# Differential attention scores: the correction product taken over 128 rows in place of 64

## The chip, the core and the metric

The kernel runs on one core of one Trainium2 chip. The metric is the device time of one execution in microseconds (us). Engines are named as in the profile: PE is TensorE's matmuls, PEld its loads of the stationary operand, DVE is VectorE, ACT is ScalarE, POOL is GpSimd, SP is the queue that issues the DMAs. Lines such as L643 are lines of the kernel before, unless it is said that they are of the changed one.

## What is computed

One layer of a streaming encoder over 1024 tokens of 1024 channels. A common projection of the normalised input feeds a convolution branch, gated linear attention, and differential attention; their gated sum goes through an output projection, and a SwiGLU follows. The change lies in differential attention alone: 8 heads, each with two score maps over 64 channels, subtracted after the softmax.

```
s  = einsum('bqhtd,bkhtd->bhtqk', qi, k) * HD ** -0.5      # t = 0, 1: two maps of a head, d = 64
s  = where(key_chunk <= q_chunk, s, -inf)                  # block-causal, chunks of 64
p  = softmax(s)
pd = p[:, :, 0] - lam * p[:, :, 1]
o  = einsum('bhqk,bkhv->bqhv', pd, v)
```

## The kernel before

Products that need more than the short matmul format (fp32r) are taken in two parts: an operand is split into an upper part `hi` (a cast on ACT) and the rest `lo` (a subtraction on DVE), and `mm3` (L114) adds hi·hi, hi·lo and lo·hi into one PSUM bank. Nearly all of PE's work is of this kind: three matmuls per step of K, each with its own load of a 128x128 stationary block, and 512 or 256 moving columns.

Token mixing walks through weight units of 256 columns (`units`, L43). A unit's projection is a generator that yields after 8 or so products; at each yield `tick` (L198) resumes other work that is due: pieces of weight splitting, convolution taps, and the attention cores. So the scores and values of head h stand on PE between the projections of the units that come after it. The times at which an attention core goes on are counted in ticks (`LAG`, `SPACE`, L63 to L65), not in us. The tile framework then sets the final order on every engine by its own cost estimates and places the semaphores, so one more instruction on one engine can move others.

`diff_qk` (L572) makes a head's operands. The 128 output channels of a projection are map 0 (rows 0 to 63, `L`) and map 1 (rows 64 to 127, `H`). For map 0 the tile `q0` holds the upper part of q in rows `L` and its lower part in rows `H`; `k0` holds the upper part of k in both halves. One product over 128 rows gives (q_hi + q_lo)·k_hi. For map 1 it is the same with the halves exchanged. The lower part of k lies in one tile `klo`: map 0's in rows `L`, map 1's in rows `H`. Four casts on ACT (L591 to L594) and two subtractions on DVE (L595, L596) make it for each half of the tokens, from one PSUM bank of the ring `pb` (four banks).

`diff_core` (L620) goes through the 8 blocks of 128 queries; block qb sees (qb + 1)·128 keys. `softmax` (L627) computes the scores of both maps: per map and stretch of columns, one product over 128 rows with `k` (L642), and a second over 64 rows that adds q_hi·k_lo (L643). Blocks 0 to 3 have one stretch a map, blocks 4 to 7 two. Then DVE masks and takes the maxima (L645 to L649), ACT the exponentials with their sums (L651, first into `p`, the second in place), DVE forms the difference `p` (L653 to L656). Later `turn` (L660) transposes it on PE (L667) and ACT copies it out (L669), and `values` (L673) multiplies with v (L678). The scores use the PSUM ring `sc`, two tiles of two banks; blocks 4 to 7 take both at once.

Of the kernel before, what the change touches and what calls it, by code (L numbers as in the profile page):

```python
# [8 lines left out]
F32R = mybir.dt.float32r  # L9
U8 = mybir.dt.uint8  # L10
AF = mybir.ActivationFunctionType
ALU = mybir.AluOpType
# [4 lines left out]
P = 128  # L17
S = 1024
# [22 lines left out]


def units():  # L43
    """Order in which the 256-column weight units are consumed."""
    out = []
    for h in range(NH):
        out += [("CV", 2 * h), ("A", h), ("V", h), ("CV", 2 * h + 1), ("OG", h)]
        if h < NH - 1:
            out += [("MG", h)]
    for j in range(ND // 2):  # L50
        out += [("DV", j), ("QK", 2 * j), ("MD", j), ("QK", 2 * j + 1)]
    out += [("MG", NH - 1)] + [("MC", u) for u in range(4)]
    out += [("PW", u) for u in range(4)]
    out += [("WO", u) for _ in range(2) for u in range(4)]
    for j in range(FT // 2):
        out += [("FG", j), ("FU", j)]
    out += [("FO", j) for j in range(FT // 2)]
    return out
# [9 lines left out]
def body(nc, tc, I, out):  # L68
    x_d, w_d, wf_d, wfup_d, par_d, lq_d, cst_d, msk_d, ffg_d, fng_d = I
    vec, act, pe, pool, sp = nc.vector, nc.scalar, nc.tensor, nc.gpsimd, nc.sync  # L70
# [7 lines left out]
    mix = tc.alloc_tile_pool(name="mix", bufs=1)  # L78
# [8 lines left out]
    one = cst[:, 2 * P:2 * P + 1].broadcast_to([P, P])  # L87
# [19 lines left out]
    def f(ap):  # L107
        return ap.bitcast(F32)
# [8 lines left out]
        pe.matmul(o, al, bh, start=False, stop=stop, skip_group_check=more)  # L117

    def rstd(dst, ss, n, width):
        """dst = (ss / n + eps) ** -0.5"""  # L120
        vec.tensor_scalar(out=dst, in0=ss, scalar1=1.0 / n, scalar2=EPS, op0=ALU.mult, op1=ALU.add)
        pool.tensor_tensor(out=dst, in0=dst, in1=mhalf[:, 0:width], op=ALU.pow)  # L122

    # ---- weights: stream of units, one ahead of its use, split in pieces behind the products
    ready = deque()
    state = {"n": 0, "gen": None}

# [44 lines left out]
    def wk(w, k, c=slice(0, 256)):  # L172
        return tuple(p[:, k % 2 * 256 + c.start:k % 2 * 256 + c.stop] for p in w[k // 2])

    # ---- work that runs behind the projections: generators, each yields after how many
    # parts of a projection (8 products) it goes on
    events, clock = [], {"now": 0, "seq": 0, "conv": 0.0}
    convq = deque()

# [26 lines left out]
    def run(gen):  # L206
        for _ in gen:
            tick()
# [3 lines left out]
            clock["now"] = max(clock["now"], events[0][0])  # L212
            resume()

    # ---- hidden state, transposed: [channel, token] in two exact parts
    def transposed(src, hh, hl, half, gcol):
        for k in range(KT):
            if half == 0 and k >= 4:
# [39 lines left out]
    def hs(half):  # L258
        return slice(half * HALF, (half + 1) * HALF)

    # ================= RMSNorm of x, transposed
    q4 = lambda name="q4": mix.tile([P, S + 32], F32, tag="q4", name=name, bufs=10)
    hset = bigset(big, "big", "h")
    xs = [q4("xt")[:, 0:D] for _ in range(NT)]
# [40 lines left out]
            if _ % 2:  # L305
                yield 1

    # ================= low-rank forget gate: rows 32 j to 32 j + 15 get h @ W_f with the
    # upper part of W_f, the next 16 rows that with its lower part
    ws = q4("ws").bitcast(F32R)  # L310
    wu, sst = ws[0:96, 0:HALF], ws[:, HALF:2 * HALF]
    fl4 = q4("fl").bitcast(F32R)
# [14 lines left out]
    spawn(x_rest(), 4)  # L327
    spawn(low_rank(1), 9)

    # ---- lambda of the differential attention, and its norm's weights  # L330
    lq = mix.tile([P, 256], F32, tag="h2", name="lq", bufs=10)
    sp.dma_start(lq, lq_d)
    lam = cpool.tile([P, 8], F32, name="lam")
# [1 line left out]
    for j in range(2):  # L335
        vec.tensor_tensor(out=lt[:, j * 64:(j + 1) * 64], in0=lq[:, j * 128:j * 128 + 64],
                          in1=lq[:, j * 128 + 64:j * 128 + 128], op=ALU.mult)
# [5 lines left out]
    vec.tensor_scalar(out=lam[:, 5:6], in0=par[:, P_DN:P_DN + 1], scalar1=0.5 * (1.0 - LAMBDA_INIT), scalar2=None, op0=ALU.mult)  # L343
    dng = lam[:, 5:6]

    # ---- gates: sigmoid(x) = (1 + tanh(x / 2)) / 2; what a gate multiplies carries the half
    def sigmoid2(out_, x):
        act.activation(out_, x, AF.Tanh, scale=0.5)

    for c0, n in ((P_DW, KT * TAPS), (P_GN, 2)):  # L350
        vec.tensor_scalar(out=par[:, c0:c0 + n], in0=par[:, c0:c0 + n], scalar1=0.5, scalar2=None, op0=ALU.mult)

    # ================= A. convolution
    csum = q4("csum")[:, 0:S]

    def conv_taps(ct, up, acc):
# [27 lines left out]
            yield  # L384
        convq.append(conv_taps(ct, up, acc[:, 0:S]))

    # ================= B. gated linear attention
    e4 = lambda name: mix.tile([P, S], F32, tag="e4", name=name, bufs=2)
    h2 = lambda name, dt=F32R: mix.tile([P, HALF], dt, tag="h2", name=name, bufs=10)
    G = {}  # L390
# [175 lines left out]
                yield 1  # L566
        del G[h]

    # ================= C. differential attention
    A = {}  # L570

    def diff_qk(h):  # L572
        w = unit()
        a = A.setdefault(h, {})
        q0, q1, k0, k1, kl = (q4(n).bitcast(F32R) for n in ("q0", "q1", "k0", "k1", "klo"))
        a.update(q=(q0, q1), k=(k0, k1), kl=kl)
        L, H = slice(0, 64), slice(64, 128)
        for half in range(2):
            c = hs(half)
            o = yield from proj_t(w, 0, half, hset)  # L580
            raw = h2("qraw", F32)
            act.activation(raw, o, AF.Copy, scale=0.125)
            act.copy(q0[L, c], raw[L])
            act.copy(q1[H, c], raw[H])
            vec.tensor_tensor(out=q0[H, c], in0=raw[L], in1=f(q0[L, c]), op=ALU.subtract)
            vec.tensor_tensor(out=q1[L, c], in0=raw[H], in1=f(q1[H, c]), op=ALU.subtract)
            yield
        for half in range(2):
            c = hs(half)
            o = yield from proj_t(w, 1, half, hset)  # L590
            act.copy(k0[L, c], o[L])  # L591
            act.copy(k1[H, c], o[H])
            act.copy(k0[H, c], o[L])
            act.copy(k1[L, c], o[H])  # L594
            vec.tensor_tensor(out=kl[L, c], in0=o[L], in1=f(k0[L, c]), op=ALU.subtract)  # L595
            vec.tensor_tensor(out=kl[H, c], in0=o[H], in1=f(k1[H, c]), op=ALU.subtract)  # L596
            yield
        spawn(diff_core(h), 2)

# [20 lines left out]
    def diff_core(h):  # L620
        a = A[h]
        osb = mix.tile([P, NT, P], F32, tag="o4", name="osb", bufs=2)
        ss = mix.tile([P, 8], F32, tag="ss", name="ss", bufs=2)
# [3 lines left out]
        def softmax(qb):  # L627
            n = (qb + 1) * P
            t = slice(qb * P, (qb + 1) * P)
            st_ = mix.tile([P, 8], F32, tag="st", name="st", bufs=4)  # L630
            p0 = e4("p")
            b0 = 0
            if n <= HALF:
                s2 = bank2().rearrange("p (a b) -> p a b", a=2)
                sc = [s2[:, i, 0:n] for i in range(2)]
            else:
                b0 = P if n == HALF + P else 0
                sc = [bank2()[:, b0:b0 + n], bank2()[:, b0:b0 + n]]
            for i in range(2):
                L = slice(64 * i, 64 * i + 64)  # L640
                for c in (slice(0, min(n, HALF - b0)), slice(HALF - b0, n))[:1 + (n > HALF)]:
                    pe.matmul(sc[i][:, c], a["q"][i][:, t], a["k"][i][:, c], start=True, stop=False)  # L642
                    pe.matmul(sc[i][:, c], a["q"][i][L, t], a["kl"][L, c], start=False, stop=True)  # L643
                if n > HALF:
                    vec.memset(sc[i][0:64, n - 64:n], NEG)  # L645
                    vec.tensor_reduce(out=st_[:, i:i + 1], in_=sc[i], axis=AX.X, op=ALU.max, negate=True)
            if n <= HALF:
                vec.memset(s2[0:64, :, n - 64:n], NEG)
                vec.tensor_reduce(out=st_[:, 0:2], in_=s2[:, :, 0:n], axis=AX.X, op=ALU.max, negate=True)  # L649
            for i in range(2):  # L650
                act.activation((p0[:, 0:n], sc[1])[i], sc[i], AF.Exp, bias=st_[:, i:i + 1],  # L651
                               accum_out=st_[:, 2 + i:3 + i])
            vec.reciprocal(st_[:, 4:6], st_[:, 2:4])  # L653
            vec.tensor_scalar(out=st_[:, 6:7], in0=st_[:, 2:3], scalar1=st_[:, 5:6], scalar2=nlam,
                              op0=ALU.mult, op1=ALU.mult)
            vec.scalar_tensor_tensor(out=p0[:, 0:n], in0=sc[1], scalar=st_[:, 6:7], in1=p0[:, 0:n],  # L656
                                     op0=ALU.mult, op1=ALU.add)
            return p0, st_
# [24 lines left out]
        pend, parts, plan = {}, {}, []  # L683
# [50 lines left out]
                sp.dma_start(g_d[2 * u + c, :, hs(half)], sg)  # L734
                yield

    # From here on the tokens go in two parts: tiles 0, 1, 4, 5 and tiles 2, 3, 6, 7
    PARTS = ((0, 1, 4, 5), (2, 3, 6, 7))

    def part(ap, i):  # L740
# [2 lines left out]
    def pair(ap):  # L743
        return ap.rearrange("p (a c) -> p a c", a=2)

    # ================= convolution: LayerNorm over channels, swish
    def conv_norm(cs):
        csum = b4("csum")
        sp.dma_start(csum, s_d)
# [70 lines left out]
                spawn(conv_norm(us))  # L820
    drain()
    spawn(conv_split(1))
    # ================= pointwise convolution, gate, sum of the branches
    yset = bigset(keep, "kb", "y")

    def pointwise(u):
# [19 lines left out]
    for u in range(4):  # L846
        run(pointwise(u))

    # ================= output projection, residual, RMSNorm
    # The SwiGLU's first product is taken in 2 x 2 blocks (output columns and tokens, halves of K)  # L850
    # by Winograd's form of Strassen's algorithm: seven block products in place of eight.
    # right operands: "11", "21", "22" (blocks of h) and T1..T4 (their sums)
    B = {}
    x2 = {}
    ffg = b4("ffg")
# [71 lines left out]
    for half in range(2):  # L927
# [2 lines left out]
                block(name, keep, "kb")  # L930
        for u in range(4):
            run(out_proj(half, u))
    # ================= SwiGLU, first product
    NU = FT
    first = state["n"]
    block("T4", keep, "kb")
# [41 lines left out]
    right = ("11", "T1", "T2", "21", "T3", "T4", "22")  # L978
# [41 lines left out]
            hilo(B["T4"][0][:, k, :], B["T4"][1][:, k, :], u)  # L1020
            yield 3

    # the second product's operands
    mids, x3 = {}, {}

    def load_mid(j):
# [21 lines left out]
    for at, (n, p) in enumerate(order):  # L1048
# [15 lines left out]
        o = ch["abacaab"[p]]  # L1064
# [33 lines left out]
    drain()  # L1098
    fbs[0].release()

    # ================= SwiGLU, second product, residual, RMSNorm
    fc = tc.alloc_tile_pool(name="fc", bufs=1)
    fng = fc.tile([P, D], F32, tag="fng", name="fng")
    sp.dma_start(fng, fng_d)
# [105 lines left out]
```

## Time and profile before

| what | value |
|---|---|
| three timed runs | 2170.72, 2171.11, 2172.71 us; median 2171.11 |
| span of the profiled execution, its own time | 2171.2 us, 0.1 above the median |
| PE busy | 2147.5 us, 99% of the span |
| DVE, ACT busy | 1385.6 us (64%), 859.0 us (40%) |
| mean granted clock of TensorE | 0.998 of full speed, which is the level of 2.4 GHz |
| products of scores | 192 of L642 and 192 of L643, between 637.6 and 1218.2 us |

The busy time of PE says that it always has something in flight, not that it is at its peak: matmuls overlap, and their ends are modelled. What a product takes from the engine is read from the step, the time from its start to the start of the next one. Two views matter: the engine's instructions in order of time, and the groups by line.

### The profile page before, as it was taken

To read this page: it belongs to the slowest core of one execution; us is meant where nothing else is said; L and a number is where in the kernel's file an instruction comes from. 1 tells how busy PE (TensorE), PEld (TensorE's weight loads), DVE (VectorE), ACT (ScalarE), POOL (GpSimd) and SP (SyncE) were. 2 spreads that over 40 slices of the span, in tenths; PEclk is the share of its full clock that TensorE was granted. 3 is DMA by queue.
4 is the path that set the end of the run, shared out by engine and by line. 5 is a ranking of instruction groups with operands and counts; after the bars stand their busy time and mean duration, and the time that the engine had idled before them with its cause. 6 is when DMAs were issued, how large, how long until landed. Compare 5 with 4: busy or idle time off the path is not lost.

```text
span 2171.2 us, 27863 instructions
## 1 busy us (share of the span) xinstructions
PE 2147.5 (99%) x10988; PEld 1787.7 (82%) x10988; DVE 1385.6 (64%) x2088; ACT 859.0 (40%) x1729; POOL 45.5 (2%) x45
## 2 busy tenths in 40 slices
PE   8999999999999999999999999999999999999998
PEld 6988988889887878778777888898888888888886
DVE  5988798789755454454545356567755545576766
ACT  6342251342345455455545354234433333341212
POOL 0000000000000000000000000000000000000000
PEclk9999999999999999999999999999999999999999
DMA  4112112121121111110111265443322222282111
GB/s 159 39 59 68 59 41 77 49 74 55 48 78 30 49 44 40 35 59 25 59 35 53 71 241 165 131 140 122 107 89 78 92 73 81 85 292 97 59 39 78
DMA packets 65059, 177.65 MB, mean 82 GB/s; under 512 B 6720, under 2 KB 17600, under 8 KB 64928
## 3 DMA queue, kind: packets, MB, share of 16 engines
q1 hardware_dynamic: 64928, 175.88, 24.4%
q8 instruction: 86, 1.41, 0.3%
q14 instruction: 45, 0.37, 0.1%
HBM read 137.58 MB, written 38.27 MB: 81 GB/s over the span
## 4 chain that ended last, share of the span: by engine, by line
PE 95%; DVE 3%; DMA 1%; issue 0%; POOL 0%; ACT 0%; SPq 0%; DVEq 0%; POOLq 0%; ACTq 0%
PE pb L115 22%; PE pb L116 22%; PE pb L117 22%; PE sc L115 6%; PE sc L116 5%; PE sc L117 5%; PE sc L643 3%; PE pb L678 3%; PE sc L642 3%; PE pb L667 1%; POOL sm L122 0%; DVE wl L112 0%; DVE xn L1127 0%; PE pb L712 0%; PE pb L504 0%
## 5 line engine op out<-in xcount | busy, mean ns | idle before, releaser
L115 PE MATMUL pb<-h,wh 128*128 128x512 f32 x1152 | 462.8, 402 | 0.0
L117 PE MATMUL pb<-h,wl 128*128 128x512 f32 x1152 | 450.9, 391 | 0.0
L116 PE MATMUL pb<-h,wh 128*128 128x512 f32 x1152 | 450.6, 391 | 0.0
L111 ACT CAST wh<-wr 128x512 fp32r<-128x512 f32 x331 | 203.5, 622 | 394.4 <-DVE x L1119 122.1
L112 DVE TENSOR_TENSOR wl<-wr,wh 128x512 fp32r<-128x512 f32 x331 | 225.5, 688 | 165.3 <-ACT wh L111 163.4
L362 DVE SCALAR_TENSOR_TENSOR acc<-up,par,acc 128x1024 f32<-128x1024 f32 x240 | 307.1, 1280 | 2.7
L115 PEld LDWEIGHTS pb<-h,wh 128*128 128x128 f32 x1152 | 217.1, 188 | 48.3 <-issue 5.1
L117 PEld LDWEIGHTS pb<-h,wl 128*128 128x128 f32 x1152 | 216.6, 188 | 46.8
L116 PEld LDWEIGHTS pb<-h,wh 128*128 128x128 f32 x1152 | 217.0, 188 | 41.3 <-DVE h L228 0.9
L1119 DVE TENSOR_TENSOR x<-x,pb 128x512 f32<-128x512 f32 x176 | 120.0, 684 | 59.8 <-PE pb L117 59.2
L115 PE MATMUL pb<-wh,h 128*128 128x256 f32 x512 | 148.1, 289 | 0.0
L117 PE MATMUL pb<-wh,h 128*128 128x256 f32 x512 | 144.9, 283 | 0.0
L116 PE MATMUL pb<-wl,h 128*128 128x256 f32 x512 | 144.8, 283 | 0.0
L115 PE MATMUL sc<-bT,wh 128*128 128x512 f32 x352 | 137.0, 390 | 0.5 <-ACT bT L111 0.5
L116 PE MATMUL pb<-wl,mh 128*128 128x512 f32 x352 | 136.9, 389 | 0.0
L115 PE MATMUL pb<-wh,mh 128*128 128x512 f32 x352 | 136.9, 389 | 0.0
L117 PE MATMUL pb<-wh,ml 128*128 128x512 f32 x352 | 136.9, 389 | 0.0
L116 PE MATMUL sc<-bT,wh 128*128 128x512 f32 x352 | 136.8, 389 | 0.0
L117 PE MATMUL sc<-bT,wl 128*128 128x512 f32 x352 | 136.6, 389 | 0.0
L111 ACT CAST wh<-s 128x512 fp32r<-128x512 f32 x88 | 54.5, 621 | 129.5 <-PE sc L116 79.4
L115 PEld LDWEIGHTS pb<-wh,h 128*128 128x128 f32 x512 | 98.1, 192 | 1.2 <-issue 0.6
L116 PEld LDWEIGHTS pb<-wl,h 128*128 128x128 f32 x512 | 98.1, 192 | 0.3
(249 smaller groups left out, 3768.2 us busy)
## 6 DMA issues: line engine op xcount, KB each, us to landing
wr<-w_dram SPq DMA_DIRECT2D x176, 512.0 KB, 3.6
m_d<-t SPq DMA_DIRECT2D x44, 256.0 KB, 2.1
mr<-m_d SPq DMA_DIRECT2D x22, 512.0 KB, 5.5
y_d<-y SPq DMA_DIRECT2D x28, 256.0 KB, 2.0
xt<-x_dram SPq DMA_DIRECT2D x8, 512.0 KB, 5.4
c_d<-acc SPq DMA_DIRECT2D x8, 512.0 KB, 2.7
g_d<-sgc SPq DMA_DIRECT2D x16, 256.0 KB, 2.1
c<-c_d SPq DMA_DIRECT2D x8, 512.0 KB, 7.8
```

Of the source, the lines that this page charges most:

```text
L111: act.copy(hi, src)
L112: vec.tensor_tensor(out=lo, in0=src, in1=f(hi), op=ALU.subtract)
L115: pe.matmul(o, ah, bh, start=start, stop=False, skip_group_check=more)
L116: pe.matmul(o, ah, bl, start=False, stop=False, skip_group_check=more)
L117: pe.matmul(o, al, bh, start=False, stop=stop, skip_group_check=more)
L362: vec.scalar_tensor_tensor(out=acc, in0=up[:, j:j + S], scalar=w, in1=acc, op0=ALU.mult, op1=ALU.add)
L642: pe.matmul(sc[i][:, c], a["q"][i][:, t], a["k"][i][:, c], start=True, stop=False)
L643: pe.matmul(sc[i][:, c], a["q"][i][L, t], a["kl"][L, c], start=False, stop=True)
L667: pe.transpose(pt[:, i * P:(i + 1) * P], pd[:, (g0 + i) * P:(g0 + i + 1) * P], ident)
L678: pe.matmul(ov[:, 0:P], parts[k // 4][:, c], a["v"][:, k, :], start=k == 0, stop=k == nk - 1)
L1119: vec.tensor_tensor(out=xx, in0=xx, in1=o, op=ALU.add)
```

## The change

For each map the lower part of k is now held in both halves of the partitions, as the upper part is, so that the second product has the same rows as the first: (q_hi + q_lo)·k_lo over 128 rows. It adds the term q_lo·k_lo to the sum. The tile `klo` (1024 columns, of the ring `q4`) is replaced by `kl0` for map 0 in the same ring, and by `kl1` for map 1, which is one tile for all heads (two halves that alternate between heads) and takes one of the three buffers of the ring `v8`; that ring otherwise holds v. DVE makes four subtractions a half of the tokens in place of two. Other edits remove comments. Lines of the changed kernel are 3 or 4 higher from L577 on: L642 and L643 are L645 and L646 there, L595 and L596 are L599 and L600, L651 is L654, L656 is L659, L669 is L672.

```
@@ def diff_qk(h):
-        q0, q1, k0, k1, kl = (q4(n).bitcast(F32R) for n in ("q0", "q1", "k0", "k1", "klo"))
-        a.update(q=(q0, q1), k=(k0, k1), kl=kl)
+        q0, q1, k0, k1, l0 = (q4(n).bitcast(F32R) for n in ("q0", "q1", "k0", "k1", "kl0"))
+        if "l1" not in A:
+            A["l1"] = mix.tile([P, 2, S], F32R, tag="v8", name="kl1", bufs=3)
+        l1 = A["l1"][:, h % 2, :]
+        a.update(q=(q0, q1), k=(k0, k1), kl=(l0, l1))
...
-            vec.tensor_tensor(out=kl[L, c], in0=o[L], in1=f(k0[L, c]), op=ALU.subtract)
-            vec.tensor_tensor(out=kl[H, c], in0=o[H], in1=f(k1[H, c]), op=ALU.subtract)
+            for to in (L, H):
+                vec.tensor_tensor(out=l0[to, c], in0=o[L], in1=f(k0[L, c]), op=ALU.subtract)
+                vec.tensor_tensor(out=l1[to, c], in0=o[H], in1=f(k1[H, c]), op=ALU.subtract)
@@ def softmax(qb):
-                L = slice(64 * i, 64 * i + 64)
...
-                    pe.matmul(sc[i][:, c], a["q"][i][L, t], a["kl"][L, c], start=False, stop=True)
+                    pe.matmul(sc[i][:, c], a["q"][i][:, t], a["kl"][i][:, c], start=False, stop=True)
```

On PE the order of products is the same, but for one product of a projection at seven places. More moves on DVE and ACT, at the same seven places: where block 7 of one head meets the k unit of the next. This is DVE there in the kernel before (`klo` the lower part of the next head's k, `sc` the scores of block 7, `wl` the lower part of a weight, `p` the difference of the maps):

```order
L645 MEMSET sc 64x64
L646 TENSOR_REDUCE st<-sc 128x1
L595 TENSOR_TENSOR klo<-pb,k_5500 64x512
L596 TENSOR_TENSOR klo<-pb,k_5501 64x512
L645 MEMSET sc 64x64
L646 TENSOR_REDUCE st<-sc 128x1
L112 TENSOR_TENSOR wl<-wr,wh 128x512 x2
L653 RECIPROCAL st<-st 128x2
L654 TENSOR_SCALAR st<-st,lam 128x1
L656 SCALAR_TENSOR_TENSOR p<-sc,st,p 128x1024
```

and the same place of the changed kernel:

```order
L648 MEMSET sc 64x64
L649 TENSOR_REDUCE st<-sc 128x1
L599 TENSOR_TENSOR kl_5507<-pb,k_5505 64x512
L600 TENSOR_TENSOR kl_5064<-pb,k_5506 64x512
L599 TENSOR_TENSOR kl_5507<-pb,k_5505 64x512
L600 TENSOR_TENSOR kl_5064<-pb,k_5506 64x512
L648 MEMSET sc 64x64
L112 TENSOR_TENSOR wl<-wr,wh 128x512
L649 TENSOR_REDUCE st<-sc 128x1
L112 TENSOR_TENSOR wl<-wr,wh 128x512 x2
L656 RECIPROCAL st<-st 128x2
L657 TENSOR_SCALAR st<-st,lam 128x1
```

Two more subtractions and one weight piece stand ahead of the second map's maximum. On ACT at the same place before (`th` are the copies of block 6's transposes, `wh` the upper part of a weight):

```order
L651 ACTIVATE p,st<-sc,st 128x1024
L111 CAST wh<-wr 128x512 x2
L651 ACTIVATE sc,st<-sc,st 128x1024
L669 COPY th<-pb 128x512
L669 COPY th<-pb 128x384
L111 CAST wh<-wr 128x512 x2
L591 CAST k_5500<-pb 64x512
```

and in the changed kernel:

```order
L654 ACTIVATE p,st<-sc,st 128x1024
L111 CAST wh<-wr 128x512 x3
L672 COPY th<-pb 128x512
L672 COPY th<-pb 128x384
L654 ACTIVATE sc,st<-sc,st 128x1024
L594 CAST k_5505<-pb 64x512
```

The exponential of the second map now stands behind one more weight cast and behind the two copies, which wait for PE's transposes of block 6.

## Rows read from the trace of the kernel before

**Rows 1.** The page's part 1: busy time of the engines in the whole span.

```profile
PE 2147.5 (99%) x10988; PEld 1787.7 (82%) x10988; DVE 1385.6 (64%) x2088; ACT 859.0 (40%) x1729; POOL 45.5 (2%) x45
```

**Rows 2.** Sums of a stretch, the attention's: length, busy PE, PEld, DVE, ACT, POOL, clock, DMA.

```profile
637.00:1225.00 588.00, 588.00 (x3060) 462.33 (x3059) 288.98 (x544) 299.60 (x730) 11.45 (x7) 1.00 0.13 43
```

**Rows 3.** The chain that ended last, same stretch, by line.

```profile
by line: PE pb L115 21.3%; PE pb L117 19.8%; PE pb L116 19.7%; PE sc L643 12.0%; PE pb L678 10.9%; PE sc L642 10.0%; PE pb L667 5.2%; PE pb L712 1.2%
```

**Rows 4.** Line L643 alone: durations (min, median, max), first and last start, widths.

```profile
L643 PE MATMUL sc<-klo,q x192: 323/440/505, 637.7 to 1218.2; 64*128 64x512 f32 x80, 64*128 64x256 f32 x48, 64*128 64x384 f32 x48, 64*128 64x128 f32 x16
```

**Rows 5.** PE in time around block 7's scores: start, duration, line, shape.

```profile
993.26 0.39 PE L117 MATMUL pb<-h,wl 128*128 128x512 f32 x1
993.49 0.39 PE L642 MATMUL sc<-k,q 128*128 128x512 f32 x1
993.81 0.49 PE L643 MATMUL sc<-klo,q 64*128 64x512 f32 x1
994.23 0.50 PE L642 MATMUL sc<-k,q 128*128 128x512 f32 x1
...
996.81 0.50 PE L115 MATMUL pb<-h,wh 128*128 128x512 f32 x1
997.14 0.40 PE L116 MATMUL pb<-h,wh 128*128 128x512 f32 x1
```

**Rows 6.** PEld in time at the same place; idle time before in brackets.

```profile
993.27 0.19 PEld L642 LDWEIGHTS sc<-k,q 128*128 128x128 f32 x1
993.81 0.18 PEld L643 LDWEIGHTS sc<-klo,q 64*128 64x128 f32 x1 [0.35 <-issue]
994.23 0.19 PEld L642 LDWEIGHTS sc<-k,q 128*128 128x128 f32 x1 [0.24 <-issue]
...
996.91 0.19 PEld L116 LDWEIGHTS pb<-h,wh 128*128 128x128 f32 x1
```

**Rows 7.** PE in time, scores of blocks 0 (128 columns) and 1 (256).

```profile
1008.14 0.32 PE L643 MATMUL sc<-klo,q 64*128 64x128 f32 x1
...
1008.91 1.83 PE L678 MATMUL pb<-dv,th 128*128 128x128 f32 x14
...
1014.41 0.28 PE L117 MATMUL pb<-wh,h 128*128 128x256 f32 x1
1014.53 0.28 PE L642 MATMUL sc<-k,q 128*128 128x256 f32 x1
1014.74 0.38 PE L643 MATMUL sc<-klo,q 64*128 64x256 f32 x1
...
1015.68 2.05 PE L678 MATMUL pb<-dv,th 128*128 128x128 f32 x16
```

**Rows 8.** Groups by line and shape, DVE: busy us, mean ns, idle before.

```profile
L596 DVE TENSOR_TENSOR klo<-pb,k 64x512 fp32r<-64x512 f32 x16 | 11.1, 695 | 0.2
```

**Rows 9.** DVE, ACT, PE in time behind block 7's scores, to its transposes.

```profile
997.22 0.69 DVE L596 TENSOR_TENSOR klo<-pb,k 64x512 fp32r<-64x512 f32 x1
1000.16 1.08 ACT L651 ACTIVATE sc<-sc,st 128x1024 f32<-128x1024 f32 x1
1001.02 0.93 PE L667 MATMUL pb<-cst,p 128*128 128x128 f32 x7
1001.66 0.97 ACT L669 COPY th<-pb 128x512 f32<-128x512 f32 x2 [0.31 <-PE pb L667]
1001.90 1.28 DVE L656 SCALAR_TENSOR_TENSOR p<-sc,st,p 128x1024 f32<-128x1024 f32 x1
1003.16 0.28 PE L115 MATMUL pb<-wh,h 128*128 128x256 f32 x1
1005.32 1.03 PE L667 MATMUL pb<-cst,p 128*128 128x128 f32 x8
```

**Rows 10.** DVE and PE in time: block 5's difference and its transposes.

```profile
977.88 1.02 DVE L656 SCALAR_TENSOR_TENSOR p<-sc,st,p 128x768 f32<-128x768 f32 x1
980.34 0.82 PE L667 MATMUL pb<-cst,p 128*128 128x128 f32 x6
```

## The prediction

> **What bounds the kernel now.** I read the page's busy times first. PE has something in flight for 99% of the span, DVE for 64%, ACT for 40% [rows 1]. The sums of the attention's stretch come next: from 637 to 1225 us PE is busy all of 588.00 us, at a granted clock of 1.00, the 2.4 GHz level, while DVE works 289 us and ACT 300 us [rows 2]. So PE sets the time here and nobody keeps it waiting. The chain, cut by line, says what PE spends it on: L642 and L643 hold 10.0% and 12.0% of 588 us, together 129 us [rows 3]. There are only 192 of each, of known widths [rows 4]. That is 0.34 us a product at a mean width of 384 columns, which is much for PE in this kernel, and the next view tells why.
>
> In PE's instructions in order of time I look at starts, not durations. A projection's product of 512 columns is followed by the next after 0.23 us (993.26 to 993.49). Among the scores the step is longer: 993.81 to 996.81 is seven products of 512, 3.00 us, so 0.429 us each. The first product of the block takes 0.32 us, and the first one behind the block, L115, 0.33 us [rows 5]. At 256 columns it is 0.12 us in a projection, and (1015.68 - 1014.74) / 3 = 0.313 us among the scores [rows 7]. The surplus, 0.20 and 0.19 us, does not depend on the width, so it is not the streaming of columns. PEld's rows show what it is: the load for the 128-row product of 993.49 starts at 993.27, one step ahead, beside a product in flight. The load for the 64-row product starts at 993.81, together with its own product, after 0.35 us of idle time, and so does the next 128-row load, at 994.23. Behind the block the loads run ahead again [rows 6]. A load lasts 0.18 to 0.19 us, about the surplus. So wherever 64 rows follow 128 or 128 follow 64, the load is not hidden.
>
> **The change on PE.** All products of a block now have 128 rows. I take it that their loads run a step ahead as in the projections, which also load the same block twice in a row for hi·hi and hi·lo. L642 and L643 together have 160 products of 512 columns, 96 of 384, 96 of 256 and 32 of 128 [rows 4], in 64 blocks. The first products of blocks are 32, 16, 8 and 8 of these, which leaves 128, 80, 88 and 24 others.
>
> - 512 columns: 128 x (0.429 - 0.23) = 25.5 us.
> - 256 columns: 88 x (0.313 - 0.12) = 17.0 us.
> - 384 columns: no row for the normal step; with the mean surplus of the two, 0.196 us, 80 x 0.196 = 15.7 us.
> - 128 columns: the step before is (1008.91 - 1008.14) / 3 = 0.257 us [rows 7]. The normal step is not shown; at most it is that of 256 columns, 0.12 us, at least what a straight line through 512 and 256 gives, 0.065 us, so the gain lies between 3.3 and 4.6 us. I take 3.3, since a short product still needs its load.
> - First products: 0.32 - 0.23 = 0.09 us, and the same at 256 columns (1014.53 to 1014.74, 0.21 us, against 0.12) [rows 5, 7]. 64 x 0.09 = 5.8 us. About half of the blocks follow transposes or values instead of a projection, which these rows don't show; without them it is 2.9 us.
> - The product behind a block: 0.33 - 0.23 = 0.10 us, 64 x 0.10 = 6.4 us, half of it if only the blocks with a projection behind them gain.
>
> The sum is 73.7 us, or between 68 and 75 us by these bounds. A cross-check: at normal steps the 384 products take 160 x 0.23 + 96 x 0.175 + 96 x 0.12 + 32 x 0.12 = 69 us, and the chain gave them 129 us; the 60 us between are the 61.5 us of the first four items.
>
> **The change on DVE and ACT.** DVE gets two more subtractions in each of 16 k halves: 32 x 0.695 = 22.2 us [rows 8]. PE's stretch hides them: DVE would be busy 311 of 514 us, ACT 300 of 514. What counts is who waits behind them. PE's bank of `pb` comes back with the last subtraction: before at 997.22 + 0.69 = 997.91, and the projection that takes it again starts at 1003.16, a margin of 5.25 us [rows 9]. Two more subtractions (1.39 us) and PE's lead of 1.58 us from block 7 leave over 2 us. The buffer of `v8` that `kl1` keeps leaves two for v; the last use of one v, in the core of its second head, comes more than a unit of projections before the next but one is written, so nobody waits.
>
> The place where it becomes tight is block 7, at seven head boundaries, where DVE's and ACT's order changes. I count from block 7's first score, 993.49. Before, the difference `p` was ready at 1001.90 + 1.28 - 993.49 = 9.69 us, and PE transposed it at 11.83 us: 2.14 us to spare [rows 9]. PE now gets there 0.09 + 7 x 0.199 + 0.10 = 1.58 us sooner, and 0.12 us later by the one product put ahead: 10.37 us. On ACT the second exponential stands behind the copies of block 6's transposes. Those came at 7.53 us, now 5.95; the copies start 0.64 us behind and take 0.97 us, so the exponential starts at 7.56 us, and from its start to the finished `p` it was 3.02 us: 10.58 us. On DVE the second maximum comes three pieces later, 3 x 0.695 = 2.1 us, and starts up to 0.7 us sooner because the first map is complete sooner. From the exponential's start at 6.67 us that makes 8.07, and `p` at 11.09 us. So PE waits 0.2 to 0.7 us where it did not wait before. I take 0.4 us, nearer to the first, since at 6.67 us the exponential itself may have been late: 7 x 0.4 = 2.8 us. The bounds are nothing and 1.4 us each (no sooner start), 9.9 us.
>
> Block 5 has 1.44 us between `p` (978.90) and its transposes (980.34) [rows 10]; PE comes 1.56 us sooner, but its scores too, so `p` moves by at least the 0.7 us of a first map. No wait.
>
> 2171.2 - 73.7 + 2.8 = 2100.3 us for the profiled execution, whose span is 0.1 us above the median of the runs: 2100 us. Its own bounds are 2171.2 - 75 = 2096 and 2171.2 - 68 + 9.9 = 2113 us.
>
> **Rivals.**
>
> *The loads stay unhidden.* Some other property of these short groups, not the rows, keeps the loads back: the scores alternate between stretches of banks and take the same stationary block twice. Then every step stays, DVE's work is hidden, and the time is 2171 us. Against it: in the projections 128-row loads run ahead although the block repeats, and the load for the first L642 ran ahead too [rows 6]. The Trainium skill ("TensorE: Matmul & The Clock Gate", Part 3, the mechanism) says that a load overlaps products in flight only where its row group is another one; by that rule equal rows gain nothing, and the time would be the 2171 us of this rival. The trace of before disagrees, since a 128-row load began at 993.27 beside a 128-row product that began at 993.26.
>
> *The gain is partly given back.* PE comes sooner everywhere, ticks are shorter, and PE begins to wait for `p` or for banks of `sc` in several blocks of a head. With 1 us at each of blocks 4 to 7 in 8 heads it is 32 us: 2171.2 - 73.7 + 32 = 2130 us. For it: the margins of 1.44 and 2.14 us are no larger than the lead of one block. Against it: the scores' own chain starts sooner by most of that lead.
>
> *VectorE becomes what PE waits for, and the kernel is slower.* The place is the bank of `pb` at the 16 k halves. If the last subtraction slid behind a whole softmax chain of 9.69 us, PE would wait 9.69 - (5.25 - 1.58) = 6.0 us each time, 96 us in all: 2171.2 - 73.7 + 96 = 2194 us. It decides from 73.7 / 16 = 4.6 us a half. Against it: only two subtractions are added ahead of that bank's return, and DVE has 40% of the stretch free.
>
> **How the numbers follow.** The forecast has 0.83, the part given back 0.09, the unhidden loads 0.05, the slower kernel 0.03. A difference of 0.2%, 4.3 us, is what a measurement of this kernel can tell from none. Faster takes the first two cases, 0.92; same 0.05; slower 0.03. The range for 8 in 10 is 2092 to 2117 us: the forecast's bounds, widened by 4 us on either side for reorderings that I did not follow.
>
> **What the changed profile would show.** Right: the second product's rows read 128x512; steps among the scores of 0.23 and 0.12 us; their loads a step ahead without idle time; the scores' share of the chain falls from 129 to about 70 us; the attention's stretch gets some 71 us shorter, the rest of the span stays. DVE's low parts of k are 64 instructions of about 0.69 us. At block 7's transposes PE shows a short wait for DVE. Wrong: steps still at 0.4 us (first rival), or PE idle before transposes, scores or projections by more than 10 us in all (the others).

## The result, and the profile after

| | before | changed |
|---|---|---|
| median of the runs beside each other | 2171.91 us (4 runs, 2170.72 to 2175.48) | 2100.35 us (4 runs, 2100.25 to 2101.18) |
| ratio to before, 95% interval | | 0.9673 [0.9659, 0.9686] |
| span of the profiled execution | 2171.2 us | 2098.6 us |
| from the first to the last L643 (L646) | 637.7 to 1218.2 us | 637.5 to 1146.1 us |

The forecast was 2100 us, with 2092 to 2117 us as the range. The span of the changed kernel lies 1.8 us below the time of the same execution (2100.38 us), so spans are compared with spans here and times with times: 72.6 us between the spans, 71.6 us between the medians.

Of the 72.6 us, 1.6 us do not belong to the change. In the profiled execution of the kernel before, the granted clock fell to half, the level of 1.2 GHz, from 1072.6 to 1076.0 us, behind block 7's scores of one head. PE was busy before (all of the 435.6 us from 637 on) and throughout, and why the clock fell is not shown. Length, PE, PEld, DVE, ACT, POOL busy, clock and DMA there:

```profile
1072.60:1076.00 3.40, 3.40 (x9) 2.60 (x9) 2.83 (x5) 1.50 (x3) 0.00 (x0) 0.50 0.00 0
```

PE's nine projection products from 1072.36 to 1076.12 us take 3.76 us there, where 0.33 + 8 x 0.23 = 2.17 us is normal behind a block. The clock of 1.00 in [rows 2] is a rounded mean that hides it; in the same stretch of the changed kernel the clock did not fall.

PE in order of time, block 7's scores of the changed kernel (its L645 and L646 are L642 and L643 of before); they answer to [rows 5]:

```profile
1017.18 0.40 PE L117 MATMUL pb<-h,wl 128*128 128x512 f32 x1
1017.41 0.39 PE L645 MATMUL sc<-k,q 128*128 128x512 f32 x1
1017.64 0.40 PE L646 MATMUL sc<-kl,q 128*128 128x512 f32 x1
1017.87 0.39 PE L645 MATMUL sc<-k,q 128*128 128x512 f32 x1
...
1019.02 0.39 PE L646 MATMUL sc<-kl,q 128*128 128x512 f32 x1
1019.24 0.40 PE L115 MATMUL pb<-h,wh 128*128 128x512 f32 x1
1019.48 0.39 PE L116 MATMUL pb<-h,wh 128*128 128x512 f32 x1
```

Eight products take 1.83 us, 0.23 us each, where they took 3.32 us before. The step of the first product and that of L115 behind the block are normal too. Its loads, in PEld's order of time, answer to [rows 6]:

```profile
1017.18 0.19 PEld L645 LDWEIGHTS sc<-k,q 128*128 128x128 f32 x1
1017.41 0.19 PEld L646 LDWEIGHTS sc<-kl,q 128*128 128x128 f32 x1
1017.64 0.19 PEld L645 LDWEIGHTS sc<-k,q 128*128 128x128 f32 x1
```

Each load now starts with the product ahead of its own, without idle time in brackets. Over all 64 blocks before, 320 of the 384 loads started together with their own product, all but the first of each block; in the changed kernel none of the 384 does. The narrow blocks, 128 and 256 columns, answer to [rows 7]:

```profile
963.99 0.28 PE L646 MATMUL sc<-kl,q 128*128 128x128 f32 x1
964.10 0.27 PE L645 MATMUL sc<-k,q 128*128 128x128 f32 x1
964.21 0.28 PE L646 MATMUL sc<-kl,q 128*128 128x128 f32 x1
964.32 1.44 PE L681 MATMUL pb<-dv,th 128*128 128x128 f32 x11
...
969.89 0.28 PE L645 MATMUL sc<-k,q 128*128 128x256 f32 x1
970.01 0.28 PE L646 MATMUL sc<-kl,q 128*128 128x256 f32 x1
...
970.36 1.95 PE L681 MATMUL pb<-dv,th 128*128 128x128 f32 x16
```

0.11 and 0.12 us a product. The chain of the shortened stretch, cut by line (its last entry is broken off in the view), and the sums of the same stretch (length, PE, PEld, DVE, ACT, POOL busy, clock, DMA), answer to [rows 3] and [rows 2]:

```profile
by line: PE pb L117 20.9%; PE pb L116 20.8%; PE pb L115 20.6%; PE pb L681 11.9%; PE sc L646 6.7%; PE sc L645 6.6%; PE pb L670 5.8%; DVE p L659 1.8%; ACT sc L654 1.6%; ACT th L672 1.3%; PE pb L715 1.2%; DVE st L657 0.4%; issue 0.3%; DVE st L
```

```profile
637.00:1152.00 515.00, 513.78 (x3053) 453.02 (x3052) 309.60 (x574) 295.81 (x729) 11.45 (x7) 1.00 0.15 49
```

The scores' share is 13.3% of 515 us, 68 us, where it was 129 us. DVE works 310 us of the stretch instead of 289, in 73 us less of it. PE, which was busy without a gap, now has 1.2 us of gaps, at block 7, and there the chain passes over DVE and ACT. Its 5% on them says where the chain runs, not what it costs; that is read from PE's steps below. PE, DVE and ACT at that place answer to [rows 9]:

```profile
1023.37 0.93 PE L670 MATMUL pb<-cst,p 128*128 128x128 f32 x7
...
1027.55 0.39 PE L115 MATMUL pb<-h,wh 128*128 128x512 f32 x1
1028.11 1.06 PE L670 MATMUL pb<-cst,p 128*128 128x128 f32 x8 [0.17 <-DVE p L659]
```

```profile
1023.67 1.23 DVE L649 TENSOR_REDUCE st<-sc 128x1 f32<-128x1024 f32 x1
...
1026.68 1.28 DVE L659 SCALAR_TENSOR_TENSOR p<-sc,st,p 128x1024 f32<-128x1024 f32 x1
```

```profile
1024.01 0.97 ACT L672 COPY th<-pb 128x512 f32<-128x512 f32 x2
1024.93 1.09 ACT L654 ACTIVATE sc<-sc,st 128x1024 f32<-128x1024 f32 x1
```

The step from L115 to the transposes is 0.56 us where 0.23 is normal. At the seven boundaries it is 0.31 to 0.37 us too long, 2.35 us in all. The brackets show only half of it: they count from the recorded end of L115's product (1027.55 + 0.39 us), which is modelled and lies behind the next normal start. The second maximum was done at 1024.90 and the copies at 1024.98, so DVE and ACT were late together.

### The profile page after: what moved, and what is told of

The parts are those of the page before. It is cut to its first block, busy times and chain, and to the rows that moved or that the text cites. A ratio compares the mean times of both kernels' runs of the same rounds, so it can differ in the third digit from the quotient of the medians.

```text
span 2098.6 us, 27902 instructions
## 1 busy us (share of the span) xinstructions
PE 2073.2 (99%) x10988; PEld 1778.7 (85%) x10988; DVE 1407.5 (67%) x2120; ACT 855.5 (41%) x1729; POOL 45.5 (2%) x45
## 4 chain that ended last, share of the span: by engine, by line
PE 93%; DVE 4%; ACT 1%; issue 1%; DMA 1%; POOL 1%; SPq 0%; DVEq 0%; POOLq 0%
PE pb L117 22%; PE pb L116 22%; PE pb L115 22%; PE sc L115 6%; PE sc L116 6%; PE sc L117 6%; PE pb L681 3%; PE sc L646 2%; PE sc L645 2%; PE pb L670 1%; POOL sm L122 1%; DVE wl L112 0%; DVE p L659 0%; DVE xn L1130 0%; ACT sc L654 0%
## 5 line engine op out<-in xcount | busy, mean ns | idle before, releaser
L115 PE MATMUL pb<-h,wh 128*128 128x512 f32 x1152 | 457.7, 397 | 0.0
L115 PEld LDWEIGHTS pb<-h,wh 128*128 128x128 f32 x1152 | 216.6, 188 | 41.7 <-ACT h L227 0.3
L115 PE MATMUL pb<-wh,h 128*128 128x256 f32 x512 | 147.2, 288 | 0.0
L115 PE MATMUL sc<-bT,wh 128*128 128x512 f32 x352 | 137.0, 390 | 0.5 <-ACT bT L111 0.5
L115 PE MATMUL pb<-wh,mh 128*128 128x512 f32 x352 | 136.9, 389 | 0.0
L115 PEld LDWEIGHTS pb<-wh,h 128*128 128x128 f32 x512 | 98.0, 191 | 0.3
```

The source lines that it names most:

```text
L115: pe.matmul(o, ah, bh, start=start, stop=False, skip_group_check=more)
```

## The experiments

Theory: a turn from a product over 128 rows to one over 64, or back, leaves one load unhidden, about 0.2 us at any width; the change removes 384 turns. Rivals: the gain comes from the new order on DVE and ACT, from where the low parts lie, or from something about 64-row loads as such. The changed kernel ran once more beside the first three.

> The changed kernel once more, beside the others on one chip. Both theories expect 2100 us, within 2 us.

Measured: 2100.73 us (2099.81 to 2101.45), ratio 0.967 [0.9655, 0.9684].

**The change's work on DVE alone.** The second product of the changed kernel goes back to 64 rows:

```
-                    pe.matmul(sc[i][:, c], a["q"][i][:, t], a["kl"][i][:, c], start=False, stop=True)
+                    L = slice(64 * i, 64 * i + 64)
+                    pe.matmul(sc[i][:, c], a["q"][i][L, t], a["kl"][i][L, c], start=False, stop=True)
```

> The changed kernel with the second product taken over 64 rows again (rows of its own half of q and of the doubled low parts); all of the change's work on DVE, and its order, stay. Theory (64-row and 128-row products in turn leave the loads unhidden): the steps among the scores are back at 0.43 us for 512 columns, DVE's 22 us are hidden, and 2171 to 2175 us come out. Rival (the gain comes from the new order on DVE and ACT, or from where the low parts lie): clearly below, 2140 us or less.

Measured: 2173.95 us (2171.8 to 2179.08), ratio 1.0013 [1.0002, 1.0023]. PE in time, block 7 (here L645 and L647):

```profile
993.69 0.40 PE L645 MATMUL sc<-k,q 128*128 128x512 f32 x1
994.01 0.49 PE L647 MATMUL sc<-kl,q 64*128 64x512 f32 x1
...
996.57 0.51 PE L647 MATMUL sc<-kl,q 64*128 64x512 f32 x1
```

From 994.01 to 996.57 six steps of 0.427 us: the surplus is back with the 64 rows, and the doubled low parts and the new order give nothing by themselves. The 22 us of added DVE work cost at most a few us (2.7 us between the medians), and in the trace PE waits for nobody in the attention. The first rival falls.

**The rows alone.** The kernel before, with one line changed; the order on every engine is that of before:

```
-                    pe.matmul(sc[i][:, c], a["q"][i][L, t], a["kl"][L, c], start=False, stop=True)
+                    pe.matmul(sc[i][:, c], a["q"][i][:, t], a["kl"][:, c], start=False, stop=True)
```

> The kernel before with the second product taken over all 128 rows of q and of the old tile of low parts. The other half of the rows then adds lower part of q times lower part of the other map's k, a term that the score should not have. The order of instructions is that of before on every engine. Theory: steps of 0.23 us at 512 columns, a gain of 73 us on PE without the seven waits at block 7, which cost 2.3 us in all: 2098 us, 2 us below the changed kernel. Rival (the low parts must lie in both halves for the gain): 2171 us.

Measured: 2097.71 us (2096.19 to 2097.86), ratio 0.9654 [0.964, 0.9669], below every run of the changed kernel beside it. A second time, beside the sixth experiment:

> The kernel with 128 rows over the shared low parts once more, beside the one with zeros on the same chip: 2098 us, and within 1 us of it.

Measured: 2097.21 us (2096.46 to 2097.29), ratio 0.9656 [0.9642, 0.9669]. So the low parts need not lie in both halves: the second rival falls. Its score holds a term of the other map, so it answers a question and is no kernel to use. The chain of the stretch up to 1150 us holds PE alone:

```profile
by line: PE pb L117 22.5%; PE pb L115 22.5%; PE pb L116 22.4%; PE pb L678 12.1%; PE sc L643 6.7%; PE sc L642 6.6%; PE pb L667 6.0%; PE pb L712 1.2%
```

**Grouped products.** The kernel before, 64 rows kept, but in each block all first products stand ahead of all second ones:

```
             for i in range(2):
-                L = slice(64 * i, 64 * i + 64)
                 for c in cols:
                     pe.matmul(sc[i][:, c], a["q"][i][:, t], a["k"][i][:, c], start=True, stop=False)
+            for i in range(2):
+                L = slice(64 * i, 64 * i + 64)
+                for c in cols:
                     pe.matmul(sc[i][:, c], a["q"][i][L, t], a["kl"][L, c], start=False, stop=True)
```

> The kernel before with the products of a block grouped: all 128-row products first, then all 64-row ones, map 0 (rows 0 to 63) before map 1 (rows 64 to 127). 64-row products stay 192. Theory (it is the turn from one row count to the other that costs): one turn a block and one behind it, 0.2 + 0.1 us, 64 x 0.3 = 19 us of the 73.7 stay, and up to 0.2 us more a block where map 1's rows follow map 0's: 2116 to 2129 us. Rival A (every load of 64 rows is unhidden, whatever stands ahead): 192 x 0.2 + 6 us stay, 2142 us. Rival B (a load overlaps only products in another row group): the steps from map 0 to map 1 are short, those within a map long, so in blocks 4 to 7 half of the 64-row steps keep 0.2 us.

Measured: 2105.11 us (2104.29 to 2105.51), ratio 0.969 [0.9675, 0.9704], faster than any of the three figures: the expectation had counted every 64-row product at a full step. PE in time, block 7 (L646 is the 64-row product; "x4" are four that follow each other), and the loads:

```profile
1021.68 1.09 PE L642 MATMUL sc<-k,q 128*128 128x512 f32 x4
1022.70 0.74 PE L646 MATMUL sc<-klo,q 64*128 64x512 f32 x4
1023.37 0.50 PE L115 MATMUL pb<-h,wh 128*128 128x512 f32 x1
1023.71 0.40 PE L116 MATMUL pb<-h,wh 128*128 128x512 f32 x1
```

```profile
1021.46 0.87 PEld L642 LDWEIGHTS sc<-k,q 128*128 128x128 f32 x4
1022.70 0.30 PEld L646 LDWEIGHTS sc<-klo,q 64*128 64x128 f32 x4 [0.37 <-issue]
1023.37 0.19 PEld L115 LDWEIGHTS pb<-h,wh 128*128 128x128 f32 x1 [0.37 <-issue]
```

Narrower windows part the groups of four: the two pairs of products, and the loads of the second pair. Below them is the one pair of block 3, with the product behind it:

```profile
1022.70 0.51 PE L646 MATMUL sc<-klo,q 64*128 64x512 f32 x2
1023.04 0.40 PE L646 MATMUL sc<-klo,q 64*128 64x512 f32 x2
...
1022.81 0.19 PEld L646 LDWEIGHTS sc<-klo,q 64*128 64x128 f32 x2
...
985.50 0.50 PE L646 MATMUL sc<-klo,q 64*128 64x512 f32 x2
985.93 0.66 PE L715 MATMUL pb<-cst,osb 128*128 128x128 f32 x4
```

Two things are to be seen. The loads wait only where the row count changes: once before the 64-row group, once behind it. And the four 64-row products of 512 columns take 0.67 us together, 0.17 us each, less than a full product. Map 0's lie in rows 0 to 63 and map 1's in rows 64 to 127, and one of each start together and run side by side. In block 3 the pair takes 0.43 us between its two turns, as long as one 64-row product took before. In block 4 the first 0.1 us of the group show it; PE's instructions from 994.48 to 994.6:

```profile
994.49 0.45 PE L646 MATMUL sc<-klo,q 64*128 64x384 f32 x2
```

Two products of 384 columns, 439 ns each by the groups by line, lie within 0.45 us. In the program, and in the order that the framework gave PE's instructions, a 256-column product of map 0 stands between them, so map 1's overtook it. Now the sum comes out: before, 73.7 us of surplus by the prediction on 384 turns, 0.19 us a turn; 128 turns stay, so 256 x 0.19 = 49 us are gone; and 192 products that take half a step, as block 3's pair suggests, save half of the 34 us that they need at the normal steps (80 x 0.23 + 48 x 0.175 + 48 x 0.12 + 16 x 0.11). 2171.2 - 49 - 17 = 2105 us. That is a span; the measured one is 2103.5 us, and the 1.6 us at the lower clock before make the difference. This is worked out after the fact, from the run that it explains. Rival A falls by the loads and the time: 64 of the 192 64-row loads run ahead, those of the second pairs. Rival B falls by the loads as well: the second pair's start at 1022.81, beside products over the same rows, and full rows overlap with full rows in the two kernels above. What is left of it is that products in the two halves of the rows overlap. 128 and 64 rows are the only counts that were run, so whether the count itself matters, or that the rows of the two products overlap only in part, stays open.

**Half of the blocks.** The kernel before, with 128 rows in blocks 4 to 7 only:

```
-                L = slice(64 * i, 64 * i + 64)
+                L = slice(64 * i, 64 * i + 64) if n <= HALF else slice(0, P)
```

> The kernel before with the second product over all 128 rows of q and of the old tile of low parts in blocks 4 to 7 only (there the score gets the further term of the other map's low part); blocks 0 to 3 keep 64 rows. Of 384 turns from one row count to the other, 128 stay. Theory (each turn costs 0.19 to 0.20 us, at any width): 96 products behind the first at 0.18 us, 32 first ones at 0.09 and 32 products behind at 0.10, 23.5 us of the gain are missing: 2097.7 + 23.5 = 2121 us. Rival (the cost grows with the columns, which blocks 4 to 7 hold nearly three quarters of): 20 us or less missing by columns, 2097.7 + 73.7 x 10240 / 36864 = 2118 us, with steps that grow with the width in blocks 0 to 3.

Measured: 2119.77 us (2119.22 to 2120.05), ratio 0.9764 [0.975, 0.9777]. The time lies between theory's 2121 and the rival's 2118 and decides nothing. The steps do. PE in time, blocks 0, 1 and 3:

```profile
976.34 0.32 PE L643 MATMUL sc<-klo,q 64*128 64x128 f32 x1
...
977.10 1.83 PE L678 MATMUL pb<-dv,th 128*128 128x128 f32 x14
...
982.93 0.38 PE L643 MATMUL sc<-klo,q 64*128 64x256 f32 x1
...
983.87 2.05 PE L678 MATMUL pb<-dv,th 128*128 128x128 f32 x16
...
995.65 0.50 PE L643 MATMUL sc<-klo,q 64*128 64x512 f32 x1
996.08 0.50 PE L642 MATMUL sc<-k,q 128*128 128x512 f32 x1
996.51 0.50 PE L643 MATMUL sc<-klo,q 64*128 64x512 f32 x1
```

Three steps of 0.253 us at 128 columns, three of 0.313 at 256, two of 0.43 at 512. Less the normal 0.11, 0.12 and 0.23 us, the surplus is 0.14, 0.19 and 0.20 us: from 256 columns on it is about a load's length (0.18 to 0.19 us) and hardly grows with them. Only at 128 columns is it less than the 0.2 us of the theory. Against 2097.71 us of the kernel with all blocks at 128 rows 22 us are missing, or 23.0 us by PE's steps among and behind the scores, where 23.5 were expected for 128 turns.

**Zeros in place of copies.** Two versions give the score no further term. In the first, one tile for both maps and all heads holds the low parts with zeros in the other half:

```
-        q0, q1, k0, k1, kl = (q4(n).bitcast(F32R) for n in ("q0", "q1", "k0", "k1", "klo"))
-        a.update(q=(q0, q1), k=(k0, k1), kl=kl)
+        q0, q1, k0, k1 = (q4(n).bitcast(F32R) for n in ("q0", "q1", "k0", "k1"))
...
+        if "low" not in A:
+            A["low"] = mix.tile([P, 2, S], F32R, tag="v8", name="klo", bufs=3)
+            vec.memset(f(A["low"][H, 0, :]), 0.0)
+            vec.memset(f(A["low"][L, 1, :]), 0.0)
+        kl = [A["low"][:, i, :] for i in range(2)]
```

> The second product over 128 rows, with the low parts of a map in its own half and zeros in the other, set once for all heads: one tile for both maps (a buffer of the ring v8), written by two subtractions a half as before, so the score gets no further term. The tile is single for all heads, so the low parts of the next head's k wait for block 7's scores. Theory (the rows of the product decide, not what lies in them): 2098 us as with the shared low parts, or up to 1 us more at each of seven boundaries, 2105 us. Rival (the gain needs data in all rows): 2171 us.

Measured: 2101.35 us (2100.89 to 2103.16), ratio 0.9682 [0.9669, 0.9695]. What the expectation says of the order is wrong: in the program the next head's subtractions for the first 512 columns stand ahead of block 7's scores, so that seven blocks read low parts of the wrong head there. That makes PE wait for DVE; who waited for whom, PE from 637 to 1140 us (total us, times, longest):

```profile
PE sc L648 <- DVE klo L600: 1.2, 7, 0.2
```

The steps are normal elsewhere, so zeros serve as well as data. The single tile has its price: PE's steps at the seven places are 3.3 us too long in all, of which the brackets show 1.2 us, and the median lies 3.6 us above the 2097.71 us of the kernel with one changed line, timed apart.

In the second, `kl0` is a tile for each head and `kl1` alternates between heads, as in the changed kernel, and GpSimd writes the zeros:

```
+            pool.memset(f(A["l1"][0:64]), 0.0)
...
+        pool.memset(f(l0[H, 0:S]), 0.0)
...
-            for to in (L, H):
-                vec.tensor_tensor(out=l0[to, c], in0=o[L], in1=f(k0[L, c]), op=ALU.subtract)
-                vec.tensor_tensor(out=l1[to, c], in0=o[H], in1=f(k1[H, c]), op=ALU.subtract)
+            vec.tensor_tensor(out=l0[L, c], in0=o[L], in1=f(k0[L, c]), op=ALU.subtract)
+            vec.tensor_tensor(out=l1[H, c], in0=o[H], in1=f(k1[H, c]), op=ALU.subtract)
```

> As the changed kernel, with two subtractions a half in place of four: each map's low parts lie in their own half of the rows, zeros in the other, written by GpSimd (one memset of 64x1024 a head for kl0, one of 64x2x1024 in all for kl1). Instruction order on PE and ACT is that of before, on DVE but for four places. Theory (row count decides; the seven waits at block 7 came from the two added subtractions and the order that they brought): 2098 us, 2 to 3 us below the changed kernel, and no wait of PE in the attention. Rival (waits come from PE being early, not from DVE's added work): 2100 us, waits at block 7 as in the changed kernel.

Measured: 2097.9 us (2095.78 to 2098.39), ratio 0.966 [0.9646, 0.9673]. PE waits for nobody in the attention, so the seven waits of the changed kernel came from the two added subtractions and the order that they brought. GpSimd's part for `kl0`, by line (busy us, mean ns | idle before):

```profile
L582 POOL MEMSET kl<- 64x1024 f32 x8 | 7.6, 949 | 372.8 <-PE sc L646 258.5 <-PE pb L504 71.5 <-issue 42.8
```

It lies on an engine that has little else to do there (11.45 us in 588 before). This version computes what the kernel before does and is the fastest of those that do, about 3 us below the changed kernel by the medians. The two were not timed side by side, and their intervals against before overlap; the kernel with one changed line, which was timed beside the changed one, is faster than it by 3 us without overlap of runs.

## Why the prediction was right, point by point

**The steps.** Forecast 0.23 us at 512 columns and 0.12 at 256; measured 0.23 and 0.12. At 128 columns 0.12 was taken as the upper bound, and 0.11 us came; the choice of that end, since a short product still needs its load, held. Added up from PE's steps, before less changed, the four items by width gave 24.9, 17.1, 15.5 and 3.4 us, 61.0 us where 61.5 were forecast. The first products gave 5.9 us (forecast 5.8) and the products behind the blocks 6.1 us (6.4), so those after transposes and values, which the prediction had left open, gained as well. That is 73.0 us of 73.7. The prediction's cross-check by the chain was none: it set 60 us for all 384 products against the 61.5 us of four items, though the first products belong to the 384 too. By steps the 384 products took 137.9 us before and 71.0 after; the chain gives them 129 and 68.

**The cause.** The loads run ahead, as the rows of PEld had suggested. That it is the turn between row counts was argued in the prediction from one sort of place; the grouped kernel and the one with half of the blocks show it. What the prediction said of single loads, about 0.2 us each, stands from 256 columns on. Why a load does not run ahead across such a turn, no run shows.

**DVE's 22 us.** Hidden, as forecast: DVE's sum in the stretch rose by 20.6 us and PE's gaps in it are 1.2 us. The bank of `pb` and the buffer of `v8` made nobody wait.

**Block 7.** Forecast: transposes due 10.37 us behind the first score, `p` ready at 10.6 by ACT or 11.1 by DVE, a wait of 0.4 us seven times, 2.8 us. Measured: due at 1027.55 + 0.23 - 1017.41 = 10.37 us, `p` at 1026.68 + 1.28 - 1017.41 = 10.55 us; seven waits, 2.35 us. The two paths came out level, ACT's estimate 0.03 us and DVE's half a us too late. The forecast chose its 0.4 us between the two.

**The sum.** 2100.3 us was forecast against a span; as a span it is 1.7 us too high (2098.6), as a time 0.05 us off. The prediction took the span for the time of the execution. For the changed kernel the two differ by 1.8 us. The other way, the execution of before that it started from held the 1.6 us at the lower clock. The two nearly cancel, so the close agreement in time is luck. The gain itself, 70.9 us, was forecast 1.7 us short by spans and 0.7 us by medians; without the 1.6 us the spans give 71.0 us.

**The rivals.** Unhidden loads: refuted by PEld's rows. Gain partly given back: only at block 7 and by 2.35 us. VectorE as the bound: the k halves cost no wait.

## What to carry to other kernels

Read the step between starts, not the durations: 480 and 495 ns against 390 looked like a little, and the steps were nearly twice the normal ones. Where products over 64 and 128 rows alternate, give all of them 128 rows, with zeros or a harmless term in the rest, or group them by row count; here the first recovered all of the surplus (73.5 us) and the second nine tenths (66.1 us). Before copying data into the second half, ask whether the rows need data at all: zeros from a nearly idle engine did the same without the new waits.

## What the runs showed that was not expected

64-row products in the two halves of the rows run side by side and out of the program's order: four of 512 columns in 0.67 us. In block 3 a pair of them takes as long as one (0.43 us), so a product over 64 rows costs half of what it does alone when its neighbour lies in the other half. Here both always wrote to different banks; the same bank was not run. At 512 columns the two turns a block, 0.2 us each, ate most of what that gave. And a turn costs no more at 512 columns than at 256 (0.20 and 0.19 us).
